# Seven-product pairs in the attention projection and in the middle of the down product of a hybrid encoder layer

## The chip, the cores and the metric

One Trainium2 chip, one of its cores. The metric is the device time of one execution in microseconds; the profile is one execution taken by the hardware profiler. TensorE (PE) does the matrix products, VectorE (DVE), ScalarE (ACT) and GpSimd (POOL) the elementwise work; SP, ACT and POOL also issue DMA transfers.

## The reference

One step of a layer over 576 tokens (512 of a new stream, 64 of a running one), model width 1024, FFN width 2816, four mLSTM heads, sixteen attention heads, all in float32:

```python
h = layer_norm(ALPHA * x + 0.5 * swiglu_ffn(x, w_gu1, w_down1))        # FFN1, LN1
z = h @ w_in     # mLSTM q, k, v, o, i, f | attention q, k, v | branch gates g_m, g_a
h = layer_norm(ALPHA * h + w_out(sig(g_m) * P_m(mLSTM(h)) + sig(g_a) * P_a(BandAttn(h))))   # LN2
y = layer_norm(ALPHA * h + 0.5 * swiglu_ffn(h, w_gu2, w_down2))        # FFN2, LN3
```

where `swiglu_ffn(x)` is `(silu(gate) * up) @ w_down` with `gate, up = split(x @ w_gu)`. The outputs are y, the convolution tails, the mLSTM states and the newest keys and values. P_a is "the projection" (`w_ap`, 1024 by 1024) below, P_m is `w_mp`, `w_out` is `w_o`.

## The kernel before

**Tiles and split products.** Activations lie with the feature on the 128 partitions and the 576 tokens along the free dimension; eight such tiles make a width of 1024 (`KT`), 22 the FFN's width (`FT`). To keep float32 accuracy each operand is split into a high and a low part, and a product is three matmuls: high by high, high by low, low by high. Weights come as tiles of 128 by 1024 (`wr`, by SP's queue). ScalarE makes the high part `wh`; VectorE makes the low part `wl` as the difference, or, for the weights listed in `ADDED`, ScalarE writes the negated high part and a DMA from POOL's queue adds the raw weights from DRAM to it (`add_lo`). `pump` keeps this going: it holds at most two raw tiles and `NWB` split pairs; `take` hands the next one of `plan`, the written order of all weights, to a product, and `done` frees it.

**Seven products.** Where two column tiles stand side by side, four blocks of the sum can be done by a Strassen-like scheme: the tokens are cut in two halves of 288, the sum dimension in two halves of four blocks, and the output in two column tiles. Seven products of four blocks replace eight. `Combos` makes the combined operands (t1 to t4) once, `Units` runs the gate and up tiles of both FFNs in this way, and `Columns`, made of it, pairs of `w_in` columns: the v and o columns of the mLSTM and the gate pairs (56, 57) and (70, 71). Pairs made beforehand lie in DRAM (`GD`, `VD`, `OD`) until they are wanted.

**Order.** The kernel runs FFN1, LN1, attention (16 heads in eight steps), six gate tiles of `w_in` (64 to 69), the projection (eight plain tiles, each multiplied by its gate and written to `MD`), four mLSTM heads, the last gate (63), `w_mp`, `w_o`, LN2, FFN2 and LN3. Each engine's instruction order is fixed when the program is built; `Order` (`od`) puts work into it by estimated times: `later(dt, fn)` runs a piece that much later, `bg` holds background generators, and `force` runs them until a condition holds. Within the mLSTM, `FILL` says which gate tiles stand behind each head as plain matmuls, between a head's last products and the point where its result `hf` is wanted.

**Down product.** In each FFN the tiles 0 and 1 run `joined` through all 22 blocks, in three loads of 8, 8 and 6 blocks (`DC`); tiles 2 to 5 follow one by one in both token halves, and 6 and 7 by halves. `Norm` takes the results (`cb`): for each tile and half it forms the residual from the high and low part of the layer's input, adds the product and keeps the running sums for mean and variance.

Of the kernel before, what the change touches and what calls it, by code (L numbers as in the profile page):

```python
# [81 lines left out]
def tile_layer(ctx: ExitStack, tc: tile.TileContext, ins, outs):  # L82
# [93 lines left out]
    FILL = ((), (58,), (), (59, 60, 61, 62))  # L176
# [22 lines left out]

    @hot(30)  # L200
    def pump(limit=2):
        while True:
            c = wst["conv"]
            if wst["dma"] < len(plan) and plan[wst["dma"]][0] in EARLY + EARLY1:
                wst["dma"] += 1
                continue
            if c < len(plan) and plan[c][0] in EARLY + EARLY1:
                if c not in parts:
                    return
                wst["conv"] += 1  # L210
                continue
            if wst["dma"] < min(len(plan), c + 2):
                i = wst["dma"]
                raws[i] = wpool.tile([P, 1024], F32, tag="wr", name=nm("wr"), bufs=2)
                src = plan[i][1]
                SP.dma_start(raws[i][:, :src.shape[1]], src)
                wst["dma"] += 1
                continue
            if c < wst["stop"] and c < wst["taken"] + limit and wst["used"] < NWB:
# [24 lines left out]
                wst["used"] += 1  # L244
                wst["conv"] += 1
                continue
            return
# [105 lines left out]

    stops = []

    def plan_ffn(n):
        for j in range(CL[n]):
            for e in range(2):
                plan.append(((f"gu{n}", j, e), ins[f"w_gu{n}"][e * FT + j]))
        stops.append(len(plan))  # L360
        order = [(j, c) for c in range(3) for j in range(2)]
        order += [(j, c) for j in (*range(2, KT), *range(LAST[n], KT)) for c in range(3)]
        for j, c in order:
            k0, nk = DC[c]
            plan.append(((f"dn{n}", j, c), ins[f"w_dn{n}"][j][:, k0 * P:(k0 + nk) * P]))
# [12 lines left out]
    plan_in(range(64, 70))  # L378
    plan += [(("ap", j), ins["w_ap"][j]) for j in range(KT)]
# [83 lines left out]
    class Norm:  # L463
        def __init__(self, xs, scale, eps, gi, final=None, keep=False):
# [5 lines left out]
            self.d0 = None  # L470
# [11 lines left out]

        def residual(self, j, hf):

            dh = self.half(j, hf)
            xh, xl = self.xs.p[j]
            stt(dh, hs(f(xh), hf), self.scale, hs(self.c0, hf), ALU.mult, ALU.subtract)
            stt(dh, hs(f(xl), hf), self.scale, dh, ALU.mult, ALU.add)
            self.prepared.add((j, hf))

        def collect(self, j, hf, ps):

            dh = self.half(j, hf)
            if j == 0:
                xh, xl = self.xs.p[j]
                stt(dh, hs(f(xh), hf), self.scale, ps, ALU.mult, ALU.add)
                stt(dh, hs(f(xl), hf), self.scale, dh, ALU.mult, ALU.add)
                self.prepared.add((j, hf))
                later(2800, lambda: self.shift(hf, dh))
            else:  # L500
# [6 lines left out]
                if j < KT - 1:  # L507
                    self.residual(j + 1, hf)

        @hot(HOT)  # L510
        def shift(self, hf, dh):
            if self.d0 is None:
                self.d0 = slot(F32R)
# [3 lines left out]
            dr = hs(self.d0, hf)  # L517
# [6 lines left out]
            self.residual(1, hf)  # L524

# [47 lines left out]
        def rows(self):  # L573

            self.gb = [slot(F32)[:, :512] for _ in range(4)]
            for i, t in enumerate(self.gb):
                SP.dma_start(t, ins["ln3"][:, i * 512:(i + 1) * 512])
# [46 lines left out]
        def apply(self, j, hf, rb):  # L624
# [9 lines left out]
            if self.final is None:  # L634
# [3 lines left out]
                if self.keep:  # L638
                    act(dh, dh, AF.Identity, bias=b_)
                    act(hs(hi, hf), dh)  # L640
# [22 lines left out]
    class Combos:  # L663
# [20 lines left out]
        def make(self, middle):  # L684
# [15 lines left out]
            for i in range(4):  # L700
                (h1, l1), (h2, l2) = self.xs.p[4 + i], self.xs.p[i]
                self.b[i].update(b11=(h1[:, a], l1[:, a]), b21=(h2[:, a], l2[:, a]), b22=(h2[:, b], l2[:, b]))
# [208 lines left out]

    def ffn(xs, n, gi, raw, final=None, prev=None):
        hh = {}
        with tc.tile_pool(name=nm("hr"), bufs=FT, side="right", reuse_waits="tile") as hr, \
# [82 lines left out]
            with tc.tile_pool(name=nm("h1"), bufs=n1, side="right", reuse_waits="tile") as h1, \  # L997
# [3 lines left out]
                ln = Norm(xs, 2.0 * ALPHA, 4.0 * EPS, gi, final, keep=final is None)  # L1001
# [339 lines left out]
    GD = {c: away("gd") for c in (0, 1, 6, 7)}  # L1341
# [16 lines left out]
    KEEP = {16: keep_v, 24: keep_o, 56: keep_g, 64: keep_g}  # L1358
    pairs = [(c, b) for c in range(0, KT, 2) for b in (16, 24)][1:] + [(0, 56), (6, 64)]
# [70 lines left out]
    for j in range(KT):  # L1430
        s = slot(F32)
        sg.append(s)
        if j > 5:
            SP.dma_start(s, GD[j])
            continue
        gemm(one(("in", 64 + j)), H, [lambda hf, ps, j=j: keep_cb(hf, ps, j)])
        if j == 3:
# [4 lines left out]
            ospool = tc.tile_pool(name="os", bufs=16, reuse_waits="tile")  # L1442
            osp = ostack.enter_context(ospool)
            OS = Act()
# [3 lines left out]
            def os_split():  # L1448
                for o_ in OT:
                    hi, lo = slot(F32R, osp, "os"), slot(F32R, osp, "os")  # L1450
                    act(hi, o_)
                    tt(lo, o_, f(hi), ALU.subtract)
                    yield None
                    OS.p.append((hi, lo))
                for s_ in sg[:4]:
                    yield act(s_, s_, AF.Sigmoid)
                osq.append(1)
                yield None

            od.bg.append((1300, os_split()))  # L1460
# [3 lines left out]
    def ap_cb(j):  # L1464
        def cb(hf, ps):
            m = hs(sg[j], hf)
            tt(m, m, ps, ALU.mult)
            if hf == 1:
                SP.dma_start(MD[j], sg[j])
                sg[j] = None  # L1470
        return cb

    for j in range(KT):
        gemm(one(("ap", j)), OS, [ap_cb(j)])
# [323 lines left out]
    gated = [0, 1, 7]  # L1798
# [5 lines left out]
    for j in range(2):  # L1804
# [125 lines left out]
```

## Time and profile before

| | us |
|---|---|
| median of 3 runs | 1571.07 (1570.38 to 1571.6) |
| profiled execution | 1571.9 |
| its span | 1570.2 |
| TensorE busy in it | 1553.9 |
| VectorE busy | 1056.0 |
| ScalarE busy | 870.1 |
| GpSimd busy | 201.1 |

The profiled execution's time is 1.7 us longer than its span. The mean granted clock of TensorE was 0.999. A row of a group reads: line, engine, operation, output and inputs by the program's names, shapes, count, then busy time and mean nanoseconds of one, then the engine's idle time in front of it and what ended that. A row of DMA issues ends with the median time from issue to landing. A row of the timeline starts with start and duration.

### The profile page before, as it was taken

To read this page: it belongs to the slowest core of one execution; us is meant where nothing else is said; L and a number is where in the kernel's file an instruction comes from. 1 tells how busy PE (TensorE), PEld (TensorE's weight loads), DVE (VectorE), ACT (ScalarE), POOL (GpSimd) and SP (SyncE) were. 2 spreads that over 40 slices of the span, in tenths; PEclk is the share of its full clock that TensorE was granted. 3 is DMA by queue.
4 is the path that set the end of the run, shared out by engine and by line. 5 is a ranking of instruction groups with operands and counts; after the bars stand their busy time and mean duration, and the time that the engine had idled before them with its cause. 6 is when DMAs were issued, how large, how long until landed. Compare 5 with 4: busy or idle time off the path is not lost. (4 is left out here: it accounts for less than half of the span.)

```text
span 1570.2 us, 29460 instructions
## 1 busy us (share of the span) xinstructions
PE 1553.9 (99%) x11743; PEld 1540.1 (98%) x11743; DVE 1056.0 (67%) x2078; ACT 870.1 (55%) x1620; POOL 201.1 (13%) x387
## 2 busy tenths in 40 slices
PE   9999999999999999999999999999999999999997
PEld 9999999999999999999999999999999999999997
DVE  7877778636798686677512667755776777786536
ACT  7545456224866687677743878653456454554222
POOL 2000000000300144434112212202111000000000
PEclk9999999999999999999999999999999999999999
DMA  9322322324854466665598655552744223213333
GB/s 256 109 108 82 108 81 68 91 75 140 225 150 140 143 159 150 154 160 148 110 262 222 163 130 130 127 152 82 205 105 89 108 82 107 83 65 98 111 90 119
DMA packets 72833, 203.66 MB, mean 130 GB/s; under 512 B 8056, under 2 KB 17912, under 8 KB 72696
## 3 DMA queue, kind: packets, MB, share of 16 engines
q1 hardware_dynamic: 59736, 161.67, 31.3%
q0 software_dynamic: 12384, 39.59, 14.9%
q8 instruction: 92, 1.51, 0.4%
q10 hardware_dynamic: 576, 0.52, 0.1%
q14 instruction: 45, 0.37, 0.1%
HBM read 177.18 MB, written 17.50 MB: 124 GB/s over the span
## 5 line engine op out<-in xcount | busy, mean ns | idle before, releaser
L128 PE MATMUL mm<-s,wh 128*128 128x288 f32 (+2 forms) x3533 | 723.0, 298 | 0.3 <-ACT s L436 0.3
L128 PEld LDWEIGHTS mm<-s,wh 128*128 128x128 f32 x3533 | 567.8, 189 | 2.7 <-ACT s L436 0.6
L128 PE MATMUL mm<-s,wl 128*128 128x288 f32 (+2 forms) x1742 | 515.4, 296 | 0.9 <-DVE wl L145 0.9
L128 PEld LDWEIGHTS mm<-s,wl 128*128 128x128 f32 x1742 | 329.0, 189 | 1.1 <-DVE wl L145 1.1
L142 ACT ACTIVATE wh<-wr 128x1024 fp32r<-128x1024 f32 (+2 forms) x144 | 144.9, 1008 | 258.4 <-PE mm L128 229.6
L145 DVE TENSOR_TENSOR wl<-wr,wh 128x1024 fp32r<-128x1024 f32 (+2 forms) x86 | 99.6, 1161 | 101.9 <-ACT wh L142 101.8
L128 PE MATMUL mm<-h,wh 128*128 128x256 f32 (+1 forms) x672 | 134.7, 294 | 0.0
L128 PE MATMUL mm<-tx,wh 128*128 128x288 f32 x563 | 116.7, 296 | 0.2 <-ACT st L142 0.2
L128 PEld LDWEIGHTS mm<-h,wh 128*128 128x128 f32 x672 | 107.6, 188 | 0.2
L128 PE MATMUL mm<-h,wl 128*128 128x256 f32 (+1 forms) x336 | 98.7, 294 | 0.0
L460 POOL TENSOR_TENSOR rs<-var,mhalf 128x2 f32<-128x2 f32 (+1 forms) x6 | 5.2, 864 | 717.1 <-DVE var L148 372.9
L145 DVE TENSOR_TENSOR wl<-wt,wh 128x1024 fp32r<-128x1024 f32 x48 | 58.7, 1224 | 52.8 <-ACT wh L727 52.8
L727 ACT ACTIVATE wh<-wt 128x1024 fp32r<-128x1024 f32 x48 | 50.8, 1059 | 78.1 <-DVE wt L145 78.0
L128 PEld LDWEIGHTS mm<-tx,wh 128*128 128x128 f32 x563 | 90.6, 188 | 0.4 <-ACT st L142 0.4
L128 PE MATMUL mm<-tx,wl 128*128 128x288 f32 x290 | 85.5, 295 | 0.0
L128 PE MATMUL mm<-tx,ah 128*128 128x288 f32 x360 | 73.9, 297 | 0.6 <-ACT st L142 0.6
L145 DVE TENSOR_TENSOR wl<-wu,wh 128x1024 fp32r<-128x1024 f32 x48 | 58.7, 1223 | 21.7 <-ACT wh L727 21.7
L142 ACT ACTIVATE h<-h 128x288 f32<-128x288 f32 x78 | 34.1, 437 | 64.5 <-DVE h L145 64.5
L727 ACT ACTIVATE wh<-wu 128x1024 fp32r<-128x1024 f32 x48 | 50.8, 1058 | 32.7 <-PE mm L128 32.2
L128 PEld LDWEIGHTS mm<-h,wl 128*128 128x128 f32 x336 | 63.0, 188 | 0.0
L145 DVE TENSOR_TENSOR wl<-ws,wh 128x1024 fp32r<-128x1024 f32 x48 | 58.5, 1219 | 3.9 <-ACT wh L727 3.8
L142 ACT ACTIVATE wl<-wh 128x1024 fp32r<-128x1024 f32 x57 | 60.2, 1057 | 0.4
(352 smaller groups left out, 3450.5 us busy)
## 6 DMA issues: line engine op xcount, KB each, us to landing
wu<-in_w_gu SPq DMA_DIRECT2D x78, 512.0 KB, 4.4
wr<-in_w_in SPq DMA_DIRECT2D x54, 512.0 KB, 4.1
wl<-in_w_in POOLq DMA_DIRECT2D x46, 512.0 KB, 6.0
wr<-in_w_dn SPq DMA_DIRECT2D x40, 512.0 KB, 3.6
wu<-in_w_in SPq DMA_DIRECT2D x18, 512.0 KB, 5.0
wr<-in_w_dn SPq DMA_DIRECT2D x20, 384.0 KB, 3.2
wr<-in_w_ap SPq DMA_DIRECT2D x8, 512.0 KB, 5.0
wl<-in_w_ap POOLq DMA_DIRECT2D x8, 512.0 KB, 7.1
```

The costliest lines, as they stand in the source:

```text
L128: PE.matmul(out, lhsT, rhs, start=start, stop=stop, **kw)
L142: return ACT.activation(out, in_, func, **kw)
L145: return (eng or DVE).tensor_tensor(out, a, b, op=op)
L460: return y, POOL.tensor_tensor(y, v, mhalf[:, :n], op=ALU.pow)
L727: self.last = ACT.activation(hi, src, AF.Copy)
```

## The change

The projection's eight tiles become four pairs, each by seven products of four blocks (`ap_pair`, `seven`). The attention output's combinations `OB` are made by `os_split` while the gate tiles run; the pool `os` grows from 16 to 32 tiles. The weights' pieces are made by `split_ds`: `a` is the first tile's raw weights, `u` and `t` are combinations, `b` is the second tile's first half. In the projection, `b`'s low part comes by the adding DMA, everything else by VectorE.

In each FFN the down tiles (2, 3) and (4, 5) become pairs (`down_pair`): the blocks 0 to 7 and 16 to 21 stay plain, the blocks 8 to 15 go by seven products with combinations made by `Inner` during the joined tiles. `Norm` takes quarter results by `take`, and the residual of these FFNs is fetched from DRAM (`away`: the input `xT` for FFN1, `XD`, written by LN2, for FFN2) instead of being made of two parts.

The gate columns 70 and 71 run plainly ahead of the projection (six plain gate tiles become eight), and 58 and 59 run as a seven-product pair with the columns behind LN1; so `FILL` loses 58 behind the second head and 59 behind the last, and the mLSTM's end loads four gate tiles from `GD` instead of two.

```diff
-    FILL = ((), (58,), (), (59, 60, 61, 62))
+    FILL = ((), (), (), (60, 61, 62))
...
+    def split_ds(c):
...
+        def put(a, t):
+            n = t.shape[1]
+            ds["hi"] = act(hi[:, a:a + n], t)
+            tt(lo[:, a:a + n], t, f(hi[:, a:a + n]), ALU.subtract)
+
+        if what == "a":
+            put(0, r1)
+        elif what == "u":
+            q = ds["q"] = [slot(F32)[:, :512] for _ in range(2)]
+            r2 = ds["u"]
+            for i in range(2):
+                tt(q[i], (r1[:, 512:], r2[:, :512])[i], r2[:, 512:], ALU.add)
+            for i in range(2):
+                put(512 * i, q[i])
+        elif what == "t":
+            q = ds.pop("q")[1]
+            for i in range(2):
+                tt(q, q, r1[:, 512 * (1 - i):512 * (2 - i)], ALU.add)
+                put(512 * i, q)
+            ds["t"] = ds["hi"]
+        elif plan[c][0][0] == "dsap":
+            act(hi[:, :512], ds.pop("u")[:, :512])
+            add_lo(lo[:, :512], hi[:, :512], plan[c][1])
+            del ds["a"]
+        else:
+            put(0, ds.pop("u")[:, :512])
+            del ds["a"]
...
-    plan_in(range(64, 70))
-    plan += [(("ap", j), ins["w_ap"][j]) for j in range(KT)]
+    plan_in(range(64, 72))
+    for j in range(0, KT, 2):
+        a, b = ins["w_ap"][j], ins["w_ap"][j + 1]
+        plan += [(("dsap", j, x), w) for x, w in (("a", a), ("u", b), ("t", None), ("b", b[:, :512]))]
...
+        @hot(HOT)
+        def take(self, j, cc, ps, op, last=False):
+            d = self.d[j][:, cc]
+            tt(d, d, ps, op)
+            if last:
+                s1, s2 = self.s1[:, cc], self.s2[:, cc]
...
+    def seven(name, j, blocks, X, Y, Z, step):
...
+        product(X, "a", 1, "b11", True, False)
+        step(1)
+        product(Y, "a", 0, "b21", True, own)
+        done(ids["a"])
+        step(2)
+        product(X, "t", 0, "t2", False, False)
+        step(3)
+        product(Z, "u", 1, "t1", True, False)
+        step(4)
+        product(X, "u", 0, "t3", False, False)
+        done(ids["u"])
+        step(5)
+        product(Z, "t", 1, "b22", False, own)
+        done(ids["t"])
+        step(6)
+        product(X, "b", 0, "t4", False, True)
+        done(ids["b"])
+        step(7)
...
+    def down_pair(n, j, hp, inner, ln):
...
+        V, W = bank()[:, :HT_], bank()[:, :HT_]
+        plain(j + 1, ((V, A, True), (W, B, True)))
+        X, Y, Z = bank("mm")[:, :HT_], bank("aux")[:, :HT_], bank("mm")[:, :HT_]
...
+        seven(f"ds{n}", j, inner.b, X, Y, Z, step)
+        plain(j, ((Y, A, False), (Z, B, False)))
...
-                for j, hl in [(j, (0, 1)) for j in range(2, LAST[n])] + [(j, (hf,)) for hf in (0, 1) for j in range(LAST[n], KT)]:
+                inner = Inner(hp_, [hh[k] for k in range(8, 16)])
+                for i in range(4):
+                    later(9000 + 2200 * i, lambda i=i: inner.part(i))
...
+                for j in DS:
+                    down_pair(n, j, hp_, inner, ln)
...
+                for j, hl in [(j, (hf,)) for hf in (0, 1) for j in range(LAST[n], KT)]:
...
-    pairs = [(c, b) for c in range(0, KT, 2) for b in (16, 24)][1:] + [(0, 56), (6, 64)]
+    pairs = [(c, b) for c in range(0, KT, 2) for b in (16, 24)][1:] + [(0, 56), (2, 56)]
...
-    for j in range(KT):
-        gemm(one(("ap", j)), OS, [ap_cb(j)])
+    def ap_pair(j):
...
+            elif n in (2, 5, 6):
+                with tc.high_priority(offset=60):
+                    o, ps = {2: (o1[:, A], Y), 5: (o2[:, B], X), 6: (o1[:, B], Z)}[n]
+                    tt(o, o, ps, ALU.subtract if n == 5 else ALU.add)
...
+        seven("dsap", j, OB, X, Y, Z, step)
+    for j in range(0, KT, 2):
+        ap_pair(j)
```

More of the change, by code (lines that the diff above doesn't have):

```diff
@@ L352, in tile_layer @@
     DC = ((0, 8), (8, 8), (16, 6))
+    DS = (2, 4)
     stops = []
@@ L524, in shift @@
             self.residual(1, hf)
+            self.shifted.add(hf)
+            if self.away is not None and hf == 1:
+                for j in range(2, LAST[1]):
+                    later(600 if j < 4 else 12000, lambda j=j: self.whole(j))
         def moments(self, j, hf, dh):
@@ L701, in make, with product @@
                 (h1, l1), (h2, l2) = self.xs.p[4 + i], self.xs.p[i]
+                self.b[i].update(b11=(h1[:, a], l1[:, a]), b21=(h2[:, a], l2[:, a]), b22=(h2[:, b], l2[:, b]))
+    def seven(name, j, blocks, X, Y, Z, step):
+        ids = {}
+        def product(ps, what, half, xk, start, stop):
+            for w in "autb":
+                if what not in ids and w not in ids:
+                    ids[w] = take((name, j, w))
+            wh, wl = parts[ids[what]]
+            for i in range(4):
+                ww = slice(half * 512 + i * P, half * 512 + (i + 1) * P)
+                xh, xl = blocks[i][xk]
+                for w, x in ((wh, xh), (wh, xl), (wl, xh)):
+                    mm(ps, w[:, ww], x, start and i == 0 and w is wh and x is xh, stop and i == 3 and w is wl,
+                       skip_group_check=True)
+                od.tick()
+        own = name == "dsap"
+        product(X, "a", 1, "b11", True, False)
[16 more added lines that the diff above has]
+        step(7)
@@ L1475, in tile_layer @@
+    od.force(lambda: not OT)
+    for j in range(0, KT, 2):
+        ap_pair(j)
+    sg.clear()
     ostack.close()
@@ L1803, in tile_layer @@
         SP.dma_start(m, d)
-    for j in range(2):
+    for j in range(4):
         sg[j] = slot(F32, sgp, "sg")
```

199 lines of the change are left out of this document (165 added, 34 removed).

## The prediction

> **What bounds the kernel now.** I read the page first, for the engines' shares, then the busy time by windows for the stretches that the change touches, then the chain, the groups by shape, the DMA issues and last the timeline of the place where I expect a loss.
>
> ```profile
> span 1570.2 us, 29460 instructions
> PE 1553.9 (99%) x11743; PEld 1540.1 (98%) x11743; DVE 1056.0 (67%) x2078; ACT 870.1 (55%) x1620; POOL 201.1 (13%) x387
> 50.00:150.00 100.00, 100.00 (x755) 99.97 (x754) 79.03 (x110) 49.03 (x80) 0.00 (x0) 1.00 0.29 102
> 310.00:350.00 40.00, 40.00 (x305) 40.00 (x304) 13.78 (x23) 8.17 (x13) 0.00 (x0) 1.00 0.28 83
> 800.00:855.00 55.00, 55.00 (x415) 55.00 (x414) 7.67 (x19) 18.92 (x20) 11.11 (x24) 1.00 0.93 242
> 1450.00:1530.00 80.00, 80.00 (x601) 80.00 (x600) 38.56 (x75) 19.52 (x29) 0.00 (x0) 1.00 0.33 101
> 1560.00:1571.00 11.00, 1.69 (x16) 1.45 (x14) 5.53 (x9) 0.16 (x2) 0.69 (x1) 0.82 0.26 96
> ```
>
> The window rows give length, then busy time of PE, PEld, DVE, ACT, POOL, then granted clock, DMA share and GB/s. TensorE is busy 1553.9 of 1570.2 us, so only 16.3 us are idle, and 9.3 of these lie in the last 11 us. In the stretches of the down products (310:350, 1450:1530) and of the attention projection (800:855) PE is busy without a gap, VectorE and ScalarE have more than half their time free, and in the projection the DMA engines are 93% busy. So a matmul removed there is worth its full time, as long as VectorE, ScalarE and the loads keep ahead of a shorter stretch. The profiled execution took 1571.9 us, 1.7 over its span and 0.8 over the median of 1571.07; the sum is made against 1571.9 and 0.8 is taken off at the end. Differences below 0.2% (3.1 us) are about what a measurement of this kernel cannot tell from no change.
>
> **What is removed: 96 matmuls.** A pair of 1024x1024-column tiles takes 2 tiles x 8 blocks x 2 halves x 3 split products = 96 matmuls; seven products take 7 x 4 x 3 = 84. The four pairs of the projection and the two pairs in each FFN (there on the middle eight of 22 blocks) make 8 pairs, 96 matmuls. The gate columns cancel: 70, 71 leave the seven-product pairs, 58, 59 enter.
>
> ```profile
> 1206.75 1.58 PE aux L128 x12
> 1222.71 1.58 PE mm L128 x12
> ```
>
> Twelve matmuls take 1.58 us, 0.132 each, so 8 x 1.58 = **-12.6 us** if nothing else becomes late. The Trainium skill, "TensorE: Matmul & The Clock Gate", section "Wait — 56ns, not 53.3ns?", gives column count over 2.4 GHz plus 2.5 ns per matmul, an estimate of 122.5 ns for 288 columns, by which the sum would be -11.8 us; the row says 131.7 ns, and the row is used.
>
> **The added work, by shape.**
>
> ```profile
> L145 DVE TENSOR_TENSOR wl<-wu,wh 128x1024 fp32r<-128x1024 f32 x48 | 58.7, 1223 | 21.7 <-ACT wh L727 21.7
> L145 DVE TENSOR_TENSOR h<-mm,h 128x288 f32<-128x288 f32 x76 | 34.5, 454 | 11.6 <-PE mm L128 11.4
> L145 DVE TENSOR_TENSOR al<-wu,ah 128x512 fp32r<-128x512 f32 x48 | 33.1, 690 | 7.3 <-ACT ah L727 3.1
> L145 DVE TENSOR_TENSOR h<-h,h 128x576 fp32r<-128x576 f32 x24 | 16.7, 754 | 0.0
> L727 ACT ACTIVATE wh<-wu 128x1024 fp32r<-128x1024 f32 x48 | 50.8, 1058 | 32.7 <-PE mm L128 32.2 <-PE aux L128 0.5
> L727 ACT ACTIVATE ah<-wu 128x512 fp32r<-128x512 f32 x48 | 30.3, 632 | 44.7 <-PE mm L128 39.3 <-PE aux L128 3.4 <-ACT h L142 1.3
> L142 ACT ACTIVATE h<-mm 128x288 f32<-128x288 f32 x74 | 29.9, 404 | 6.8 <-PE mm L128 5.0
> ```
>
> *Down pairs.* Per pair VectorE gets the weight pieces (a 1.22, and nine 512-wide steps for u, t and b at 0.69: 7.4), four plain loads of at most 1.22 (4.9), ten outputs of 0.45 and four moments of two 0.45 steps (8.1): 20.4 us. PE needs 84 + 168 = 252 matmuls, 33.2 us. ScalarE gets 1.06 + 5 x 0.63 + 4 x 1.06 + 4 x 0.40 = 10.1. The operand combinations are made beside the joined tiles: four parts of four half-width steps and two 576-wide splits, 4 x (4 x 0.45 + 2 x 0.75) = 13.2 us of VectorE, beside 13.78 of 40 already there. The seven products' results are taken in 0.45 us each while the next product runs for 1.58. All of this is covered, and I cost it at nothing; if the cover failed, every product boundary could show up to 0.45. The residual now comes by eight loads per FFN instead of from two halves, which saves one VectorE step each; six are queued on SP after the last weights of the gate part and two on ACT's queue. In that stretch the DMA share is 0.28 to 0.33, so they cost nothing either. LN2's added writes of its result (sixteen half-tiles on SP) stand ahead of FFN2's loads, behind a share of that size too: 0 to 0.5, taken as 0. So the FFNs keep their part: four pairs, -6.3 us.
>
> *Projection.* Per pair VectorE gets 1.22 (a), eight steps of 0.69 (u, t), four of 0.45 and one of 0.75 for outputs and gates: 9.7 us; PE's pair now lasts 84 x 0.132 = 11.1. ScalarE gets 1.06 + 4 x 0.63 + 2 x 0.63 (b's high and negated part) + 3 x 0.40 = 6.0. Before, POOL's DMA did the low parts and VectorE had 7.67 of 55. Totals fit, but order decides: t's first half (sum 0.69, split 0.63, low part 0.69, with hand-overs about 2.2) must be there two products, 3.2 us, after the pair begins, and stands on VectorE behind the last outputs of the pair before (0.75 + 0.45 + 0.45). Walking the built order of instructions with these durations I find no wait in the first pair, about 0.5 us in the second, 1.5 in the third, and 1.7 at t in the fourth: **+3.7 us**. From below: nothing, if the splits start as soon as the raw weights land; from above: 1.7 plus a late low part of 0.9 in each of the four, less that last one: 9.5.
>
> **The loads behind it.** A pair's b is a 512-wide half whose low part comes by an adding DMA from POOL's queue, the only DMA-made part left in the pair. The first columns of the mLSTM (in 8, in 9) load after it into the buffers that u and a leave.
>
> ```profile
> wr<-in_w_in SPq DMA_DIRECT2D x54, 512.0 KB, 4.1
> wl<-in_w_in POOLq DMA_DIRECT2D x46, 512.0 KB, 6.0
> wr<-in_w_ap SPq DMA_DIRECT2D x8, 512.0 KB, 5.0
> wl<-in_w_ap POOLq DMA_DIRECT2D x8, 512.0 KB, 7.1
> tx<-h POOLq DMA_DIRECT2D x10, 288.0 KB, 4.5
> wr<-in_w_mp SPq DMA_DIRECT2D x8, 512.0 KB, 3.5
> L142 ACT ACTIVATE wl<-wh 128x1024 fp32r<-128x1024 f32 x57 | 60.2, 1057 | 0.4
> DMA to landing us min/median/max: 5.2/6.2/8.8
> ```
>
> The last row is that of all 57 adding DMAs of 512 KB. In the last pair let T be the end of the first t split. b's split on ScalarE comes next (0.63) and frees u's buffer; b's low part: two ACT steps, 1.3, then the adding DMA of 256 KB. The nearest row is 288 KB in 4.5, the ends are 3.5 and 7.1: it lands at T + 5.9, wanted at T + 0.7 + 33 x 0.132 = 5.0. **+0.9 us** (0 to 2.5). For in 8: load issued at T + 0.75, landed + 4.1, high part + 1.06, negated copy + 1.06, hand-overs 0.3, adding DMA + 6.2: T + 13.5. PE wants it 60 matmuls after t, at T + 0.7 + 7.9 + 0.9 = 9.5. **+4.0 us**; with a load of 3.5 and a landing of 5.2 it is 2.4, with 5.0 and 8.8 it is 7.5. Before, this chain was hidden, because plain tiles of 6.3 us each follow one another with the loads two ahead. in 9 goes through the same engines 2.1 us behind in 8 and is wanted 6.3 later, so it costs nothing. On SP, the writes of the gated tiles of the third pair stand ahead of this load; they wait for VectorE's products, which are done before T. Behind the adding DMA that waits for its negated copy, POOL holds only the next adding DMAs, and nobody else waits for it.
>
> **One gate less behind the last head.** FILL's last group loses column 59. The timeline of before shows what that column did:
>
> ```profile
> 1043.81 0.28 PE L128 MATMUL aux<-ch,qsc 128*64 128x258 f32 x1
> 1044.13 0.38 ACT L142 ACTIVATE hf<-aux 64x258 f32<-64x258 f32 x1 [1.57 <-PE aux L128]
> 1044.54 0.17 DVE L148 SCALAR_TENSOR_TENSOR dn<-hf,tcol 128x5 f32<-128x5 f32 x1 [1.30 <-ACT hf L142]
> 1046.02 1.21 POOL L460 TENSOR_TENSOR mrs<-var,mhalf 128x5 f32<-128x5 f32 x1 [19.33 <-DVE var L152]
> 1047.46 1.23 DVE L145 TENSOR_TENSOR wl<-wr,wh 128x1024 fp32r<-128x1024 f32 x1
> 1048.61 1.70 DVE L152 TENSOR_SCALAR hf<-hf,mv,mrs 128x256 f32<-128x256 f32 x5
> 1051.21 1.25 PE L138 MATMUL aux<-ident,hf 128*128 128x128 f32 x10
> PE aux L138 <- ACT hf L142: 1.8, 2, 0.9
> ```
>
> The last hidden-state matmul ends at 1044.1; its copy, the denominators, POOL's power, a weight split and five scalings follow until 1050.31; the ten transposes start at 1051.21, because 54 matmuls (six of a gate, then 48 of the next) stand in between. After the change only the six are left: PE is through at 1044.9, and waits for the scalings, whose order on VectorE is unchanged, the weight split included. The last five transposes (half of 1.25) end at about 1051.0, where before ten ended at 1052.46 and 48 more matmuls had been done, 24 of 256 and 24 of 320 columns, 6.4 us by 0.132 per 288. Loss: 6.4 - 1.46 = **+5.0 us** (4.5 to 5.5; the 48 matmuls themselves stand elsewhere now). Likewise the gate behind the second head is gone; heads without one wait for `hf` 0.9 each in the last row, so 0.1 to 0.9: **+0.4**.
>
> **Sum.** -12.6 + 3.7 + 0.9 + 4.0 + 5.0 + 0.4 = +1.4 on 1571.9, or 1573.3; less 0.8, **1572.5 us**.
>
> **The rivals.** *The gain stays (chance 0.27).* VectorE starts the splits early enough that the projection's pairs wait nowhere, b lands at 3.5 and the hand-over costs its low end: -12.6 + 0 + 0 + 2.4 + 4.9 + 0.2 = -5.1, 1566.0. For it: 25% of VectorE's time and 45% of ScalarE's is free in the pairs, and the loads have less to share the DMA engines with than in 800:855. Against it: the order on VectorE is fixed, and outputs stand ahead of t. *VectorE's order decides in the projection (0.25), slower.* With 9.7 us of work in 11.1 and two round trips to ScalarE inside u and t, VectorE does not catch up between pairs, and t and b are late in all four: 9.5 in place of 4.6 for the two, 4.9 more: 1577.4. It decides from the point where waits between its fourteen steps add 1.4 us to the 9.7, 0.1 for each. For it: u and t alternate between the two engines eight times, and ScalarE's queue holds output copies between them. Against: the one hand-over shown, from the copy's end at 1044.51 to `dn` at 1044.54, is 0.03, and in the window 50:150, seven products of the first FFN, VectorE is busy 79% without a gap on PE. *The clock (0.10), slower.* In the last window the granted clock is 0.82 over 11 us in which PE works 1.69, so 2.0 us of clock are lost by idleness, and nowhere else before is PE idle for long. Two new idle gaps of 4 to 5 us, if each cost as much in the work behind it, add 4.0: 1576.5. Against: the tail's gap is over 9 us. The Trainium skill, "TensorE: Matmul & The Clock Gate", section "Part 1: The HAM clock gate (the “warmup” mystery)", states that the clock halves after at least one idle window of some 3.4 us, and speaks so against this change; this trace shows the fall only in its tail.
>
> **How the numbers follow.** The forecast, a change lost in the new waits, has 0.36; its own range is 1568 to 1574.2. With the rivals' 0.27, 0.25 and 0.10, and 0.02 for anything else, halved between no change and slower, faster by over 0.2% (below 1567.9) has 0.27, within it 0.37, slower (above 1574.2) 0.36. The range takes in the fast rival's 1566.0 and the slow one's 1577.4: 1566 to 1578.
>
> **What would show it.** PE's busy time down by about 12.6 and its idle time up from 16.3 to about 30. PE's waits should name `hf` by VectorE's scaling with one of some 4 us, the low part `wl` by DMA with one of about 4 at the first mLSTM column, and `wl` or `wh` of the projection with 1 to 2 each. The down stretches should have no new wait. I am wrong if in 8 lands before PE wants it, if a filler stands behind the last head after all, if waits appear inside the down pairs, or if the clock drops below 1.0 around the two gaps.

## The result, and the profile after

The changed kernel is slower: 1584.68 us median (1582.59 to 1591.71, six runs) beside 1571.34 (1570.38 to 1574.91) for the kernel before in the same series, a ratio of 1.0093 with a 95% interval of 1.0079 to 1.0107. That is 13.3 us more, where +1.4 was forecast, and it lies above the range. The profiled execution took 1583.39 us, 11.5 more than the profiled one before; the ledger below is made against these two.

The page of the kernel after, its span and busy times:

```profile
span 1581.7 us, 29584 instructions
PE 1549.6 (98%) x11647; PEld 1531.4 (97%) x11647; DVE 1123.7 (71%) x2190; ACT 904.8 (57%) x1696; POOL 210.4 (13%) x399
```

There are 96 matmuls fewer, yet PE's busy time fell by 4.3 us only, not 12.6. About 4.0 of the difference are matmuls at half clock (below). Most of the rest lies at breaks in PE's stream of matmuls, of which this trace has 45 and the one before 29, for a break costs more than the idle time that is shown. At 847.47, where the idle time is 0.71 us, 1.02 us pass from the start of the matmul before it to its own start, and 0.24 to the start of the next, where 0.13 each is usual: 0.28 more than the 0.71. By that, an estimate, 16 further breaks are about 4 us. Idle time rose from 16.3 to 32.1, close to the 30 that was named. The waits of PE in the kernel after (total, times, longest):

```profile
PE mm L128 <- DMA wl<-in_w_in: 4.2, 1, 4.2
PE aux L138 <- DVE hf L152: 4.2, 1, 4.2
PE mm L128 <- ACT wh L142: 3.1, 3, 1.3
PE aux L138 <- DVE kwl L148: 2.0, 1, 2.0
PE aux L138 <- ACT hf L142: 1.8, 2, 0.9
PE mm L128 <- DMA wl<-in_w_ap: 1.4, 2, 0.7
PE aux L128 <- DVE s L145: 1.3, 1, 1.3
```

The two long waits are the two that the prediction sized at 4.0 and 5.0: in 8's low part by DMA, and `hf` behind the last head. Not foreseen are `kwl` at the first head, and, at LN1, `s` and the longest of the three for `wh`. The windows over the two long gaps (length, busy time of PE, PEld, DVE, ACT, POOL, granted clock, DMA share, GB/s):

```profile
864.00:866.00 2.00, 0.00 (x0) 0.00 (x0) 0.00 (x0) 1.14 (x2) 0.83 (x2) 1.00 0.87 227
866.00:868.00 2.00, 0.83 (x5) 0.83 (x6) 0.00 (x0) 0.00 (x0) 1.70 (x6) 0.86 1.04 327
868.00:870.00 2.00, 2.00 (x11) 2.00 (x11) 0.00 (x0) 1.45 (x2) 1.58 (x7) 0.50 1.07 254
870.00:872.00 2.00, 2.00 (x15) 2.00 (x15) 0.24 (x2) 1.05 (x2) 1.56 (x6) 0.79 1.04 291
1061.00:1063.00 2.00, 0.01 (x1) 0.04 (x1) 1.87 (x4) 2.00 (x4) 0.06 (x1) 0.75 0.00 0
1063.00:1065.00 2.00, 2.00 (x8) 1.44 (x9) 1.68 (x5) 0.10 (x1) 0.00 (x0) 0.50 0.63 186
1065.00:1067.00 2.00, 2.00 (x11) 2.00 (x10) 1.77 (x5) 0.00 (x0) 0.00 (x0) 0.50 1.00 356
1067.00:1069.00 2.00, 2.00 (x12) 2.00 (x11) 2.00 (x4) 0.00 (x0) 0.00 (x0) 0.54 0.83 299
```

PE is busy in 868 to 870, but does 11 matmuls in 2 us where at full clock it does 15 or 16: the granted clock is 0.50. Behind the second gap it stays there until almost 1069.

The ledger: the same events in both traces, and how far the one after is behind.

| event | before | after | shift |
|---|---|---|---|
| start of the mLSTM columns behind LN1 (`z` cleared) | 397.44 | 397.44 | 0.0 |
| last product of the attention | 778.5 | 779.4 | +0.9 |
| first matmul of the projection | 799.2 | 812.8 | +13.6 |
| its last | 850.3 | 862.4 | +12.2 |
| first head's first copy | 853.5 | 871.6 | +18.1 |
| first head's `mrs` | 915.4 | 935.4 | +20.0 |
| last head's `mrs` | 1046.0 | 1059.9 | +13.9 |
| end of the last transposes | 1052.46 | 1065.79 | +13.3 |
| first products of FFN2's gate part | 1176.58 | 1191.39 | +14.8 |
| end | | | +11.5 |

Two gate tiles stand ahead of the projection now (12.7 us) and are paid back behind the heads (6.3 and 6.4). What is lost shows in four places: FFN1, whose 3.2 us of matmuls never reach the line behind LN1; the hand-over from the projection to the first head, where about 8 us go; the tail of the last head; and the clock behind both gaps.

### The profile page after: what moved, and what is told of

It reads as the page before. It is cut to its first block, busy times and chain, and to the rows that moved or that the text cites. A ratio compares the mean times of both kernels' runs of the same rounds, so it can differ in the third digit from the quotient of the medians.

```text
span 1581.7 us, 29584 instructions
## 1 busy us (share of the span) xinstructions
PE 1549.6 (98%) x11647; PEld 1531.4 (97%) x11647; DVE 1123.7 (71%) x2190; ACT 904.8 (57%) x1696; POOL 210.4 (13%) x399
## 4 chain that ended last, share of the span: by engine, by line
PE 81%; DVE 7%; issue 4%; ACT 4%; DMA 3%; POOL 1%; ACTq 0%; SPq 0%; DVEq 0%; POOLq 0%
PE mm L128 65%; PE aux L128 13%; PE aux L138 2%; DMA wr<-in_w_in 1%; DVE wl L145 1%; DVE s L145 1%; ACT wh L142 1%; DMA wr<-in_w_ap 1%; DVE U L148 1%; DVE s L148 1%; ACT s L142 1%; DMA wr<-in_w_dn 1%; ACT L142 0%; DVE sc L1458 0%; DMA s<-s 0%
## 5 line engine op out<-in xcount | busy, mean ns | idle before, releaser
L128 PE MATMUL mm<-s,wh 128*128 128x288 f32 (+2 forms) x3661 | 751.9, 299 | 3.3 <-ACT wh L142 2.3
L128 PEld LDWEIGHTS mm<-s,wh 128*128 128x128 f32 x3661 | 590.7, 190 | 6.6 <-issue 2.4
L128 PE MATMUL mm<-s,wl 128*128 128x288 f32 (+2 forms) x1806 | 535.6, 297 | 4.4 <-DMA wl<-in_w_in 4.2
L128 PEld LDWEIGHTS mm<-s,wl 128*128 128x128 f32 x1806 | 342.5, 190 | 4.9 <-DMA wl<-in_w_in 4.4
L128 PE MATMUL mm<-h,wh 128*128 128x256 f32 (+2 forms) x384 | 78.3, 295 | 0.0
L190 POOL DMA_DIRECT2D s<-s x16 | 13.7, 854 | 481.4 <-DVE h L145 457.9
L128 PEld LDWEIGHTS mm<-h,wh 128*128 128x128 f32 x384 | 61.5, 188 | 0.2
L145 DVE TENSOR_TENSOR ws<-wu 128x1024 f32<-128x1024 f32 x48 | 58.3, 1214 | 0.0
L128 PEld LDWEIGHTS mm<-tx,ah 128*128 128x128 f32 x360 | 57.3, 188 | 0.9 <-ACT st L142 0.8
L128 PE MATMUL mm<-h,wl 128*128 128x256 f32 (+2 forms) x192 | 56.4, 294 | 0.0
```

The source lines that it names most:

```text
L128: PE.matmul(out, lhsT, rhs, start=start, stop=stop, **kw)
L145: return (eng or DVE).tensor_tensor(out, a, b, op=op)
L190: return POOL.dma_start(lo, src, accum_op=ALU.add)
```

## The experiments

The theory now was: the two long waits are as forecast, and three things come on top: the clock behind the gaps, waits at the end of FFN1, and DMA engines that are full behind the projection. The rivals were that the projection's own order loses the gain, or that the clock alone explains the difference. The times of the kernel before were 1571.34, 1571.23 and 1570.66 in the three series, and each ratio below is to that of its own series.

**Which FFN pairs pay.** Kernel *e4_down* is the kernel before with the down pairs of both FFNs, and *e5_ffn2* the same with FFN2's alone (one of the lines in which they differ):

```diff
-        for j in DS:
+        for j in (DS if n == 2 else ()):
             order += [(j + 1, 0), (j + 1, 2)] + [(j, x) for x in "autb"] + [(j, 0), (j, 2)]
```

> Only the down pairs of both FFNs; gate columns, fillers and the projection are those of the kernel before. Theory (the loss lies in the projection, the hand-over and the tail; the first FFN gains nothing, the second 3.3): 1571.3 - 3.3 = 1568.0, with no gap over 2 us and the clock at 0.999. What my prediction had for the down pairs, with both FFNs gaining 3.2: 1565.0. Rival (the down pairs are a loss by their own loads and writes): 1572 or more.

> Only FFN2's two down pairs; all else is the kernel before. Theory (the second FFN keeps its 24 matmuls of 0.132 us, the first one's were lost at the hand-over to the w_in columns, where a gap of 1.5 us also lowered the clock in some executions): 1571.3 - 3.2 = 1568.1, with no gap at the hand-over that the kernel before hasn't, and runs that scatter no more than those of before. Rival (the down pairs lose in FFN2 too, by the writes of LN2's result and the eight fetches): 1571 or more.

Both FFNs: 1570.34 (1565.69 to 1573.97, ten runs), ratio 0.9986 (0.9973 to 0.9999). FFN2 alone: **1568.21** (1566.96 to 1568.91, eleven runs), ratio 0.9978 (0.9970 to 0.9987), faster than both kernels of this case. So FFN2's pairs bring 3.0 of the 3.2 us of their 24 matmuls, without a new wait of over 0.5 us, and FFN1's bring nothing more in the median: by the ratios the kernel with both is 1.3 us slower than that with one, by the medians 2.1, though the intervals overlap. The trace of *e4_down* shows why. Its timeline, and then its windows:

```profile
398.41 0.50 PE L128 MATMUL mm<-s,wh 128*128 128x256 f32 x2 [1.53 <-ACT wh L142]
```

```profile
396.00:398.00 2.00, 0.88 (x8) 0.68 (x6) 0.49 (x1) 0.27 (x1) 1.80 (x5) 1.00 1.08 390
398.00:400.00 2.00, 1.37 (x9) 1.17 (x10) 1.61 (x4) 1.62 (x4) 0.26 (x2) 1.00 0.64 257
400.00:402.00 2.00, 2.00 (x12) 1.60 (x12) 1.15 (x3) 0.29 (x2) 0.00 (x0) 0.71 0.13 39
402.00:404.00 2.00, 2.00 (x10) 2.00 (x11) 1.05 (x3) 0.57 (x2) 0.51 (x1) 0.50 0.98 393
404.00:406.00 2.00, 2.00 (x12) 2.00 (x11) 1.44 (x2) 1.91 (x2) 2.00 (x3) 0.50 0.27 109
406.00:408.00 2.00, 2.00 (x12) 2.00 (x12) 2.00 (x5) 1.97 (x3) 1.31 (x2) 0.59 0.75 256
```

Up to LN1 part of the gain is there: `z` is cleared at 395.64, beside 397.44 in the kernel before and 397.04 in *e5_ffn2*. At 398 the first column behind LN1 waits 1.53 us for its weight split, PE is busy 2.25 us of four, and then the clock is halved for 6.8 us, which costs 3.4. The same place in *e5_ffn2*, where FFN1 runs as before:

```profile
398.00:400.00 2.00, 1.75 (x14) 1.55 (x14) 2.00 (x4) 1.50 (x4) 1.80 (x4) 1.00 0.83 260
402.00:404.00 2.00, 2.00 (x18) 2.00 (x19) 1.24 (x4) 0.17 (x1) 1.41 (x2) 1.00 0.91 301
```

The kernel after had gaps there as well (1.5 us of idling in 398 to 402, beside 1.75 in 396 to 400 of *e4_down* and 0.9 in 398 to 402 of the kernel before), and in its profiled execution the clock did not fall; in that of *e7_ogin8* (below), whose FFN1 is the same, it did (mean 0.57 in 400 to 412). The runs of *e4_down* go with their mean clock: the five of 0.998 and more took 1565.7 to 1570.1, that of 0.997 1570.55, those of 0.996 and less 1570.9 to 1574.0. The median of the first five, 1566.9, is 1.3 less than that of *e5_ffn2*: where the clock stays up, FFN1's pairs seem to bring something too. Their loss is thus waits, in the two traces, and the clock in some executions.

**What a gap costs.** Kernels *e10_gap2* and *e11_gap8* are the kernel before with one deliberate gap in the middle of its projection: a matmul that waits for a chain of ScalarE copies, with two steps in the loop below, or eight.

```diff
     for j in range(KT):
+        if j == 4:
+            gap_x = slot(F32R)
+            ps = bank()[:, :512]
+            mm(ps, OS.p[0][0][:, :P], OS.p[0][0][:, :512], True, True)
+            act(gap_x[:, :512], ps)
+            for _ in range(2):
+                act(gap_x[:, :512], f(gap_x[:, :512]))
+            ps = bank()[:, :512]
+            mm(ps, gap_x[:, :P], OS.p[0][0][:, :512], True, True)
+            act(gap_x[:, :512], ps)
```

> The kernel before with a deliberate idle gap on TensorE in the middle of its plain projection, where TensorE is busy without a break: one small matmul, a chain of three ScalarE copies of 512 columns that starts from it, and a matmul that reads the last. Nothing else waits. The gap is about 2.1 us. Theory (a gap costs its length, and from some length on the clock falls behind it): 2.1 and in some executions 1 to 2 more, 1573.5 to 1575.5. Rival (the clock falls only behind gaps of over 3.4 us): 1573.5 in every execution, clock as before.

> The same with nine copies, a gap of about 5.5 us. Theory (the granted clock falls to half while TensorE is idle and stays there some 3 to 7 us after it is busy again): 5.5 for the gap and 1.6 to 3.4 for the clock, 1578.5 to 1580.3; a window behind the gap shows 0.50. Rival (the low clock of the changed kernel has nothing to do with idleness): 5.5 only, 1576.8, clock 1.00 behind the gap.

A weight split of 1.05 us came in between on ScalarE, so the gaps were longer than meant: 3.37 and 7.34 us. The times: 1576.76 (1575.10 to 1578.69, five runs; ratio 1.0038, 1.0023 to 1.0052) and 1581.04 (1578.89 to 1582.55, four runs; 1.006, 1.0045 to 1.0075), so 6.1 and 10.4 us more. The timeline of *e10_gap2*, its windows, and then the windows of *e11_gap8*:

```profile
827.43 0.50 PE L128 MATMUL aux<-os,s 128*128 128x512 f32 x1 [3.37 <-ACT s L142]
```

```profile
828.00:830.00 2.00, 2.00 (x15) 2.00 (x14) 0.00 (x0) 0.57 (x1) 0.00 (x0) 0.69 0.90 147
830.00:832.00 2.00, 2.00 (x11) 2.00 (x11) 0.00 (x0) 0.00 (x0) 0.00 (x0) 0.50 0.70 139
832.00:834.00 2.00, 2.00 (x15) 2.00 (x15) 0.42 (x1) 0.00 (x0) 0.00 (x0) 0.96 0.03 4
```

```profile
828.00:830.00 2.00, 0.00 (x0) 0.00 (x0) 0.00 (x0) 1.90 (x4) 0.00 (x0) 0.63 0.93 168
830.00:832.00 2.00, 0.73 (x2) 0.64 (x3) 0.00 (x0) 1.19 (x2) 0.00 (x0) 0.50 0.53 104
832.00:834.00 2.00, 2.00 (x11) 2.00 (x10) 0.00 (x0) 0.60 (x1) 0.00 (x0) 0.50 0.03 8
834.00:836.00 2.00, 2.00 (x13) 2.00 (x13) 0.00 (x0) 0.00 (x0) 0.00 (x0) 0.66 0.00 0
```

The time at half clock follows from these rows, since (1 - clock) / 0.5 is the share of a window spent there: 1.24 + 2 + 0.16 = 3.4 us behind the short gap, 1.48 + 2 + 2 + 1.36 = 6.8 around the long one. The short gap costs 3.4 of idling, 1.7 of clock and some 0.9 for its two matmuls (0.40 and 0.50 in the timeline), 6.0 of the 6.1 measured. In the long one the low stretch begins while PE is still idle; what lies behind the gap costs about 2 us of clock, and with the two matmuls that makes 2.9 of the 3.1 us by which the 10.4 exceed its 7.3. Both show the low clock at idling alone, in a kernel without the change.

**Does the clock explain the rest?** Kernel *e1_busy* is the kernel after with 30 matmuls of no use at each of the two gaps (behind the projection, and behind the last head).

```diff
+    def keep_busy(n):
+        ps = bank("mm")[:, :HT_]
+        for i in range(n):
+            mm(ps, H.p[0][0][:, :P], H.p[1][0][:, :HT_], i == 0, i == n - 1)
```

> The changed kernel with thirty extra matmuls of 288 columns, whose result nobody reads, put on TensorE at each of the two places where it stood idle for 4.2 us: in front of the first mLSTM column, and behind the last gate of the last head. No work is taken away and no wait is shortened. Theory (idleness lowers the clock): TensorE has no gap there, the granted clock stays at 1.00 where it was 0.50, and though 60 matmuls (7.9 us) are added, the time falls by the clock's share, 1.6 + 2 to 3 us, to about 1579 to 1580, and the runs scatter less than the 1582.6 to 1591.7 of the changed kernel. Rival (the low clock comes from something else, or costs nothing because the waits end last anyway): 1583 to 1585, the clock still falls. Rival (the extra matmuls delay the work behind them): 1587 or more.

Measured: 1586.69 (1582.22 to 1590.77, four runs), ratio 1.0096 (1.0074 to 1.0117): no better than the kernel after. The mean clock of the profiled execution was 0.999 (0.995 to 0.997 in the other three) and both gaps were full, with 7.9 us of added matmuls in place of 8.4 of idling. But the waits went elsewhere; the last row is the window over the longest:

```profile
PE aux L138 <- DVE vl L145: 3.5, 1, 3.5
PE aux L138 <- ACT qf L142: 3.2, 2, 2.6
894.00:902.00 8.00, 4.53 (x35) 4.24 (x34) 4.66 (x13) 7.69 (x21) 2.40 (x9) 1.00 0.55 110
```

`vl` and `qf` are operands of the first head. ScalarE, which has a part in making both, stood 4.07 us waiting for the load of C0 just before (its copy starts at 884.60); how much of the two waits is that load, and how much ScalarE's own order of work, was not told apart. So the clock alone doesn't explain the difference: with the gap at in 8 filled, PE waits a little later. And not every long wait lowers the clock: here one of 3.5 us did not.

**Behind the projection: one cause, or the next in a row?** Kernel *e3_in8* lets VectorE make the low parts of in 8 and in 9, without the adding DMA. Kernel *e6_og* issues the loads of `og` behind the first state C0 instead of ahead of it, and *e7_ogin8* does both.

```diff
-... | {("in", c) for c in (*range(32), *range(56, 72))} \
+... | {("in", c) for c in (*range(8), *range(10, 32), *range(56, 72))} \
```

```diff
-            SP.dma_start(st["og"][e], OD[2 * h + e])
...
+        for e in range(2):
+            act(st["og"][e][:, 0:1], c0[:, 0:1])
+            SP.dma_start(st["og"][e], OD[2 * h + e])
```

> The changed kernel with the low parts of the first two mLSTM columns made by VectorE (one step of 1.22 us) instead of ScalarE's negated copy and an adding DMA (1.06 and about 6 us). Theory (this chain sets the wait behind the projection): the wait of 4.2 us for the low part falls to 0, the clock does not drop there, so 4.2 + 1.6 = 5.8 us less, about 1578. Rival (the raw load is the late one): most of the wait stays, now for VectorE's low part, 2 to 4 us, and the time is 1581 to 1583.

> The changed kernel, in which each mLSTM head's two og tiles (288 KB each) are loaded only once that head's state C0 has landed (a one-column copy from C0 into the tile makes the load wait), instead of all eight within 13 us behind the projection. Theory (the projection's larger pool of split operands keeps the og buffers closed until it ends, and the eight loads then delay C0 and the first columns): C0 lands 5 us earlier, the wait for kwl goes from 2.0 to below 0.5, and the time falls by 2 us to about 1582.5; the wait of 4.2 for the first column's low part stays, as its load is issued before those. Rival (kwl's wait comes from the order on ScalarE and VectorE alone): 2.0 stays, 1584 to 1585.

> As the one before, and the low parts of the first two mLSTM columns by VectorE. With the low part alone the wait only moved from the first column (4.2) to C0 (5.3 for qf, 2.8 for kwl). Theory (two chains side by side, the adding DMA and the og loads ahead of C0, each good for about 5 us): now both are gone, no wait over 1 us between the projection and the first head, 4.2 + 2.0 and the clock's 1.6 less, about 1577. Rival (a third thing ends there, such as the raw loads for the q columns): the waits at that place still sum to 4 or more, 1581 to 1585.

The times: *e3_in8* 1586.55 (1584.54 to 1588.98, four runs; ratio 1.0096, 1.0081 to 1.0111), *e6_og* 1590.64 (1590.17 to 1591.97, four; 1.0126, 1.0112 to 1.0140), *e7_ogin8* 1591.95 (1586.60 to 1598.43, four; 1.0122, 1.0098 to 1.0145). None is better than the kernel after, all three lie above both times that were expected, and *e6_og* is slower than the kernel after, its interval lying above that kernel's. Part of this is the clock: ahead of the last microseconds it is halved for 17 us in the trace of *e6_og* and for 34 in that of *e7_ogin8* (its slowest run), beside 10.2 in the kernel after. The waits of *e3_in8* and the row of ScalarE's copy of C0:

```profile
PE aux L138 <- ACT qf L142: 5.3, 1, 5.3
PE aux L138 <- DVE kwl L148: 2.8, 1, 2.8
886.25 0.64 ACT L142 ACTIVATE ch<-c 128x516 fp32r<-128x516 f32 x1 [6.82 <-DMA c<-in_C]
```

The wait for in 8 is gone, and 5.3 us for `qf` stand in its place, behind the copy of C0, which has waited 6.82 us for its load. In *e6_og* C0 was issued 8 us earlier, at 870.55, but took 12.2 us to land, at 882.7, no earlier than in the kernel after (issued at 878.80, 3.8 to land). The waits were 4.9 for in 8 and 3.5 for `vl`; in *e7_ogin8* they were 2.8 for `kwl` and 2.4 for `qf`. That `og` alone holds C0 up is thus refuted. That C0 and the weights, which are in flight together, hold each other up is likely, but not shown by these runs.

Kernel *e9_quarter* tests the sum of what is moved: the kernel after, but of the weights of columns 8, 9, 0 and 1 only a quarter is loaded and added. Three quarters of these weights are left out of the product's data; the matmuls are the same.

```diff
+                if plan[i][0] in QUARTER:
+                    src = src[:, :256]
+                    POOL.memset(raws[i][:, 256:], 0.0)
                 wst["load"] = SP.dma_start(raws[i][:, :src.shape[1]], src)
...
+                                act(lo, f(hi), scale=-1.0)
+                                added[plan[c][0]] = POOL.dma_start(lo[:, :256], plan[c][1][:, :256], accum_op=ALU.add)
```

> The changed kernel, which loads only a quarter of the weights of the first head's four columns (8, 9, 0, 1), raw and adding DMA alike; the rest is zeros, so three quarters of these weights are left out of the result. Instructions on TensorE, ScalarE and VectorE stay. Theory (behind the projection the DMA engines are full, with 6.5 MB to move in 22 us, because the pairs hold both raw buffers and all four split pairs until their end and nothing can be loaded ahead): 3 MB less, the waits of 4.2 and 2.0 fall to under 1 together, the clock stays up, about 1576 to 1578. Rival (the chain of load, split, copy and adding DMA is late by its own steps, whatever the bytes): the first wait stays above 2, 1581 to 1584.

Measured: 1574.41 (1572.44 to 1579.97, ten runs), ratio 1.0024 (1.0014 to 1.0033), about 10 us less than the kernel after. The wait for `in_w_in` is gone, none for `vl` or `qf` has come in its place, and `kwl` is down to 0.7. The same window, first in the kernel after, then in *e9_quarter*:

```profile
862.00:884.00 22.00, 17.79 (x124) 17.54 (x123) 3.82 (x8) 9.89 (x14) 7.64 (x23) 0.92 1.02 294
```

```profile
862.00:884.00 22.00, 22.00 (x170) 21.95 (x169) 9.34 (x17) 14.24 (x31) 8.46 (x29) 1.00 1.03 317
```

PE works all 22 us at full clock now. The DMA engines are full in both, so a full engine by itself is no wait; the pieces that PE wants come sooner. SP's rows show when they are issued, the kernel after first, then *e9_quarter*:

```profile
853.55 8.86 SPq L259 DMA_DIRECT2D wr<-in_w_in  x4
864.52 5.41 SPq L259 DMA_DIRECT2D wr<-in_w_in  x2
870.52 0.48 SPq L1832 DMA_DIRECT2D og<-od  x1
878.80 0.42 SPq L1874 DMA_DIRECT2D c<-in_C  x1
```

```profile
861.30 1.31 SPq L263 DMA_DIRECT2D wr<-in_w_in  x2
868.36 1.38 SPq L1840 DMA_DIRECT2D og<-od  x1
869.78 0.42 SPq L1882 DMA_DIRECT2D c<-in_C  x1
```

C0 is issued at 869.78 instead of 878.80. The shorter loads also land sooner themselves (128 KB in 2.4 us, beside 5.6 for 512 KB in the kernel after, in the median), so the run shows that the bytes of these weights make the waits, and not how much of that is their own way and how much the other transfers. In the kernel before `og` was loaded ahead of the projection and C0 issued at 852.55:

```profile
788.54 1.35 SPq L1575 DMA_DIRECT2D og<-od  x3
800.77 0.39 SPq L1575 DMA_DIRECT2D og<-od  x1
852.55 0.41 SPq L1617 DMA_DIRECT2D c<-in_C  x1
```

**The tail.** Kernel *e2_seven* has seven plain gate tiles ahead of the projection instead of eight (64 to 69 and 58, with 70 and 71 back in a pair), and so four, 59 to 62, behind the last head.

```diff
-    FILL = ((), (), (), (60, 61, 62))
+    FILL = ((), (), (), (59, 60, 61, 62))
...
-    plan_in(range(64, 72))
+    plan_in((*range(64, 70), 58))
```

> The changed kernel with the gate columns dealt out otherwise: 70, 71 go back into the seven-product pair, seven plain gate tiles (64 to 69 and 58) stand in front of the projection instead of eight, and 59 to 62 stand behind the last head. Theory (the tail's wait is the missing filler): the wait for hf goes from 4.2 to 0 and the clock stays up there, 5 us for the wait and 2 to 3 for the clock, so about 1576 to 1577. Rival (the cover is only moved): with one gate tile less in front of the projection its combined operands are late; they were finished 7.8 us before the projection began and a tile is 6.3, so up to 1 us, and if their making is delayed too, 5 us, which leaves 1579 to 1582.

Measured: 1580.30 (1576.26 to 1584.53, five runs), ratio 1.0052 (1.0032 to 1.0072), 4.4 less than the kernel after. That is where the rival put it, but not by the rival's way, for PE does not wait at the projection's start: the waits for in 8 (3.4) and `kwl` (2.7) stay, and the clock still falls at both. The wait for `hf` by VectorE's scaling is gone, and the window 1040 to 1060 has PE busy throughout:

```profile
1040.00:1060.00 20.00, 20.00 (x159) 19.99 (x158) 9.54 (x30) 7.72 (x16) 1.20 (x1) 1.00 0.16 41
```

**All of it together.** Kernel *e8_all* keeps the projection's pairs and joins to them FFN2's pairs alone, the seven gates, VectorE's low parts for in 8 and in 9, and the late `og`.

> Everything mended that the runs named: pairs in the projection and in FFN2 only, seven plain gate tiles ahead of the projection and four behind the last head, first two mLSTM columns' low parts by VectorE, og loads behind C0. Theory: of the kernel before 3.2 (FFN2) and 1.4 (what the projection kept of 6.3) come off, 0 to 2 are paid for waits left in the projection's cover: 1567 to 1569. Rival (the projection's pairs cost more than they save whatever stands around them): 1570 to 1574, slower than the FFN2 pairs alone.

Measured: 1577.99 (1576.06 to 1579.35, five runs), ratio 1.0042 (1.0030 to 1.0055), above both times that were expected. The projection's pairs are not worth keeping in this form: *e5_ffn2*, which leaves them out, is 9.8 us faster by the difference of its median. `qf` still waits 3.4 us and `kwl` 3.2:

```profile
PE aux L138 <- ACT qf L142: 3.4, 3, 2.5
PE aux L138 <- DVE kwl L148: 3.2, 1, 3.2
```

## Why the prediction was wrong

*Right: the price of a matmul.* FFN2's pairs gave 1568.21 and -3.0 in *e5_ffn2* for 24 matmuls, priced at -3.2, with "costed at nothing" holding there. The interval of that ratio, 2.0 to 4.7 us, is too wide to test the price to a few per cent.

*Right: the projection.* It lasts 49.8 us instead of 51.2. Of 6.3 us of matmuls 4.9 are lost, where 4.6 (3.7 and 0.9) were forecast; 2.9 of them are idle time and the rest goes at its breaks. By the starts of the matmuls the four pairs lose about 0, 0.7, 1.9 and 2.5, where 0, 0.5, 1.5 and 2.6 were forecast, though half of the third pair's loss is `b` and not `t`. (VectorE's 9.7 us per pair count five half-width steps; the sentence names four.)

*Right in size: in 8's low part* (4.2 us of wait, 4.0 forecast) *and the tail* (4.2 of wait; 5.0 of loss forecast, and *e2_seven*, which puts the filler back, gains 4.4).

*Wrong: "So the FFNs keep their part".* The cover was checked inside FFN1's down stretch, and not at its end. With a shorter stretch, LN1's sums (a wait of 1.35 us in the profile after) and the first weights behind it (1.3) are late, two waits of 0.4 for `s` appear inside the stretch (306.46 and 340.42), and the 3.2 us are gone in the ledger's first row. *e4_down* beside *e5_ffn2* shows the same without the other parts: nothing gained in the median, and a clock that falls in some executions.

*Wrong: "The clock (0.10)".* The prediction had the right rival and gave it too small a chance. It held against it that the tail's gap is over 9 us long; one of 3.37 already costs 1.7, and one of 1.53 with short ones beside it 3.4. The landmarks give 1.7 us behind the first gap (18.1 less 12.2 and the wait of 4.2) and 2.3 behind the second: 0.8 up to the end of the transposes (13.3, where 13.9 - 6.4 + 5.0 = 12.5 was due) and 1.5 from there to FFN2. That is 4.0 in all, the rival's own price; the forecast of +1.4 holds none of it. The scatter goes with the clock too: the kernel after ran from 1582.59 at a mean clock of 0.995 to 1591.71 at 0.990, and 0.005 of 1581.7 is 7.9 us. The Trainium skill, "TensorE: Matmul & The Clock Gate", section "Part 1: The HAM clock gate (the “warmup” mystery)", has two clock states for one busy core and a free-running window of about 3.4 us that decides between them; the low stretches of 3.4 and 6.8 us agree with that, while the fall behind 1.53 us of waiting, with PE busy 2.25 of four microseconds, shows that no wholly idle window was needed here.

*Wrong: "The loads behind it".* This step followed one load (in 8) on engines that were as free as in the trace before. It did not follow what else is moved: `og`'s eight loads of 288 KB came at 788.5 to 800.8 before, and come at 870.5 to 883.0 after, behind the weights. Their pool opens only where the projection's pools close, and the change both doubles one of these (`os`) and lets the pairs write into another (`o1` and `o2` in `op`); which of the two keeps the loads back was not tried. The load of C0 is issued 26 us later, 12 of which are the projection's own later end, and behind the first wait stands a second (`kwl`, 2.0). In the kernel after this second wait is not C0's; ScalarE's rows show what it is:

```profile
877.28 1.06 ACT L142 ACTIVATE wh<-wr 128x1024 fp32r<-128x1024 f32 x1 [5.29 <-DMA wr<-in_w_in]
878.25 0.48 ACT L142 ACTIVATE R<-mm 128x256 f32<-128x256 f32 x2
885.52 0.66 ACT L142 ACTIVATE ch<-c 128x516 fp32r<-128x516 f32 x1
```

A weight split waits 5.29 us for its raw weights, and the copy of the first column's result (`R`), which PE had finished by 875.1, stands behind it on ScalarE; VectorE's work up to `kwl` follows from that copy. C0 is copied at 885.52 without a wait. It is waited for where the waits before it are shorter or gone: 6.82 us in *e3_in8*, 4.07 in *e1_busy*, 2.73 in *e2_seven*. What *e1_busy*, *e3_in8*, *e6_og* and *e8_all* have in common is that changing one of these waits only brings out the next, 6 to 8 us in the two longest behind the projection in each; *e9_quarter*, which takes away bytes, removes them. That part is shown. It does not show whether the plain loads or the adding DMAs weigh more in it, since it shortens both.

The sum of the misses against the forecast, in the profiled execution: FFN1 3.2, attention 0.9, projection and in 8 about 0.5, the clock 4.0, `kwl` 2.0, less 0.4 for a wait that did not come: 10.2, beside the 11.5 less 1.4, or 10.1, to be explained. Of the 0.9 in the attention 0.6 are idle time at its start (1.5 us in 398 to 402, where the kernel before had 0.9); the rest was not followed. In which places the slowest runs of the kernel after lose their further 8 us of clock stays open, since only the profiled execution has a trace. That of *e7_ogin8*, at a mean clock of 0.988, has low stretches behind LN1, twice at the first head, at the tail and near FFN2's end.

## What to carry to other kernels

Price a wait of TensorE at its length and the clock that falls behind it: here 1.7 to 3.4 us more behind most waits of 3 us or longer (none behind the 3.5 of *e1_busy*), at times also for 1.5, so a saving of 3 us in matmuls can be lost by one new gap. Where a stage is made shorter or takes more buffers, list every transfer that its buffers held back or let through before, and ask whether the stage behind still finds its loads landed; a covered stretch is judged at its end, not in its middle. Try the parts of such a change singly: here FFN2's pairs alone were faster (1568.21 us), FFN1's brought nothing in the median, and the projection's with their gates lost more than both could bring.

## What the runs showed of the hardware

Every window here reads as a mix of two clocks, 1.00 and 0.50, and the low one lasts 3.4 us or a multiple of it: 3.4 behind in 8's gap and in *e10_gap2*, 6.8 around the tail's gap, in *e11_gap8* and in *e4_down*, and 10.2 in *e3_in8* (mean 0.57 in 890 to 902). The two low stretches of the kernel after start at 867.44 and 1062.0, 57 times 3.41 us apart. So it may be a gap's place on that step, and not its length alone, that decides whether the clock falls; no run tests it. In *e4_down* it fell where PE had been busy for 2.25 of four microseconds; at the same place of the kernel after, with 2.47 of four, it did not, nor behind the 3.5 us of *e1_busy*. And a DMA share of 1.02 or 1.03 went with 4.2 us of waiting in one kernel and with none in another: the share does not tell whether PE waits.
